# A fused decoder block: first loads on two queues, x's rows ahead of mem's, mem's squares on DVE, the position bias's product in the warm-up

## The chip, the cores and the metric

The kernel runs on one core of one Trainium2 chip. Its time is device microseconds of one execution; the median of three runs is what counts. A core has five engines that run their own instruction streams and wait for each other by semaphores: TensorE (PE, matrix products), VectorE (DVE), ScalarE (ACT), GpSimd (POOL) and SyncE (SP, which here only issues DMAs). ACT and POOL can issue DMAs too, on queues of their own.

## The reference

One layer of a decoder for 256 tokens of width 1024 (all float32). Only its beginning matters here: the memory's normed rows feed one product for keys and values, and the table of position biases is made from `rel_bias`.

```python
h = rmsnorm(x, g_pre_mix[l])
proj = h @ w_in[l]
(cb, cc, cv, q, k, v, qm, ga, gb, gc) = jnp.split(proj, IN_OFFSETS, axis=-1)
y_a = (cb * causal_dwconv(cc * cv, conv_mix_w[l])) @ w_conv_out[l]
o = moba_attention(to_heads(q), to_heads(k), to_heads(v), rel_bias)   # logits + bias of the distance
y_c = memory_attention(qm, rmsnorm(mem, g_mem[l]), w_mem_kv[l]) @ w_mem_out[l]
...                                                                   # gated merge, w_out, sandwich norm
u = causal_dwconv(h @ w_up[l], ffn_conv_w[l], ffn_conv_b[l])
f = (jax.nn.gelu(a) * g) @ w_down[l]
```

## The kernel before

Every float32 operand of a product is split in two parts, a rounded high part (ACT writes it, `wh`, or the first half of `memT`, `hT`, `mv`, `mk`) and the rest (DVE writes it, `wl`, or the second half). A product then takes three matmuls: high by high, high by low, low by high. The weights stream from DRAM in pieces of at most 128 x 1024 in the order in which they are used (`weight_pieces`); `split_until(n)` splits the pieces up to n, which first loads them, and `weights()` hands out the next one. Pieces w0 to w7 are the eight 128 x 512 slices of the memory's value weights, w8 to w11 the four column blocks of its key weights (128 x 1024 each), w12 to w15 the value weights of x.

The start, up to about 50 us, runs as follows.

- PE warms up on a constant (`keep_warm`, `pw`). The transposed memory `memT_in` is loaded into `rawT`, scaled by its gain `gm` and split (`mem_part`, `memT`), and `values` multiplies it with w0 to w7 into `pmv`: 48 matmuls. The memory's norm is applied afterwards, when `pmv` is copied out to `mv`, since it is one number for each token.
- The rows of `mem` and `x` (`m_sb`, `x_sb`, two tiles of 128 tokens each) are loaded for their norms alone. `rstd_full` squares and sums a row on ACT, in two halves (line 279, `junk`), and POOL adds them and takes the power -1/2 (lines 282 to 284), which gives `rm` and `rx`.
- `blocks` multiplies `memT` with w8 to w11 into two tiles `ft`, two blocks of 24 matmuls to a tile: blocks 0 and 1 in the first, 2 and 3 in the second. The keys' norm runs along the free axis, so `diagonals` puts `rm` on a diagonal (`dg`), a product with ones spreads it over all partitions (`sp`), and DVE copies it out as `rms`.
- `xn` is x times `rx`; PE turns it (`tp`), ACT and DVE scale and split it (`hT`), and `values` multiplies it with w12 to w15 into `pv`.
- The position bias: `bk`, a table of 33 x 384 with a one for the bucket of each distance, times `rb` gives `pb` (line 467); DVE copies it to `brow`, POOL writes it to DRAM (`bd`) and reads it back in a skewed form (`bias`), which the attention needs from about 73 us on.

The order of the work on PE, ACT and DVE up to the split of w11 and the order of the loads on SP's queue are written out by hand (`manual_schedule`); behind that a scheduler orders each engine's instructions when the kernel is built. SP issues its loads strictly in order, and each load first waits until the one eight places before it has landed.

Of the kernel before, what the change touches and what calls it, by code (L numbers as in the profile page):

```python
# [19 lines left out]
P = 128  # L20
# [4 lines left out]
H = 8  # L25
# [75 lines left out]
def trunk(ctx, tc, x, mem, memT_in, weights_in, par_in, rel_bias, g_post_mix, g_post_ffn, buckets, out):  # L101
# [28 lines left out]
    rawT = sb.tile([P, KT, S], F32, tag="G", name="rawT")  # L130
    par = const.tile([P, 60 + 8 * NFB], F32, name="par")
    gm, gp, gf, bg, cw = par[:, 0:8], par[:, 8:16], par[:, 16:24], par[:, 24:48], par[:, 48:60]
    fw = par[:, 60:].rearrange("p (a b) -> p a b", a=2)
    bk = sb.tile([P, 1024], F32, tag="z", name="bk")[:NB + 1, :TOEP]
    with tc.manual_schedule(engines={mybir.EngineType.Activation}):
        nc.scalar.dma_start(par[:, :8], par_in[:, :8])
    rb = const.tile([NB + 1, H], F32, name="rb")
    ident = const.tile([P, P], F32, name="ident")
    ones = const.tile([P, P], F32, name="ones")
# [147 lines left out]
    def rstd_full(src, name):  # L287
        return list(mean_square([src[:, :512], src[:, 512:]], name))[-1]

    def diagonals(rs):  # L290
        dg = wk.tile([P, NT, P], F32, tag="dg", name="dg", bufs=1)
        for t in range(NT):
            nc.vector.tensor_scalar_mul(dg[:, t], ident, rs[t])
        return dg

    def spread(dg, name):

        p = bank("sp")
# [91 lines left out]
    memT = sb.tile([P, 2, KT, S], F32R, tag="A", name="memT")  # L390
    mv = sb.tile([P, 2, NT, CW], F32R, tag="E", name="mv")
    pv = acc("pmv")

    def values(pv, a, k, wh, wl):
        for t in range(NT):
            mm_ktile([(pv[t], 0)], wh, wl, a[:, 0, k, tok(t)], a[:, 1, k, tok(t)], k == 0, k == KT - 1)

    with tc.manual_schedule(engines={mybir.EngineType.SP}):
        for what in "m01 w0 m12 w1 m24 w2 w3 m46 w4 w5 m68 w6 w7 w8 t0 w9 t1 x0 w10 x1 w11 w12 w13".split():
            if what[0] == "m":  # L400
                ks = slice(int(what[1]), int(what[2]))
                nc.sync.dma_start(rawT[:, ks], memT_in[:, ks])
            elif what[0] == "w":
                load(int(what[1:]), int(what[1:]))
            else:
                t = int(what[1])
                nc.sync.dma_start((x_sb if what[0] == "x" else m_sb)[:, t], (x if what[0] == "x" else mem)[tok(t)])
        nc.sync.dma_start(par[:, 8:], par_in[:, 8:])
        nc.sync.dma_start(rb[:NB], rel_bias)
        nc.sync.dma_start(bk, buckets)  # L410
    with tc.manual_schedule(engines={mybir.EngineType.PE, mybir.EngineType.Activation, mybir.EngineType.DVE}):
        nc.scalar.activation(small("preload"), mhalf, AF.Exp)
        pw = bank("pw")

        def keep_warm(n):
            one = nc.const_aps.tensor(1.0, (P, 512), BF16)
            for _ in range(n):
                nc.tensor.matmul(pw, one[:, :P], one, start=True, stop=True)

        def mem_part(k):  # L420
            hilo(memT[:, 0, k], memT[:, 1, k], rawT[:, k], gm[:, k:k + 1])

        keep_warm(9)
        for k in range(2):
            mem_part(k)
# [37 lines left out]

    pb = bank("pb")
    nc.tensor.matmul(pb[:H, :TOEP], rb, bk, start=True, stop=True)
    brow = wk.tile([H, TOEP], F32, tag="e", name="brow", bufs=EB)
    nc.vector.tensor_copy(brow, pb[:H, :TOEP])
    bd = dr.tile([H, TOEP], F32, name="bd")  # L470
# [382 lines left out]
```

## Time and profile before

| | us |
|---|---|
| median of 3 runs | 450.21 (449.69 to 450.3) |
| the profiled execution, its own time | 449.86 |
| its span, first to last instruction | 448.1 |
| PE busy | 435.7 (97%) |
| DVE busy | 358.2 (80%) |
| ACT busy | 292.4 (65%) |
| POOL busy | 15.6 (3%) |
| mean granted TensorE clock | 0.997 |

The span is what the trace covers; 1.76 us of the execution lie around it. Lines such as L256 are those of the kernel printed above.

### The profile page before, as it was taken

How to read it: one execution, taken by the hardware profiler on the slowest of the kernel's cores; microseconds unless marked ns; L12 is line 12 of the kernel's file. 1: busy time of each engine (PE TensorE's matmuls, PEld its weight loads, DVE VectorE, ACT ScalarE, POOL GpSimd, SP SyncE). 2: the span in 40 equal slices, each digit the busy share in tenths (PEclk: the TensorE clock that was granted, in tenths of full speed). 3: DMA queues.
4: the chain of work that ended last, by engine and by line, in shares of the span. 5: the costliest groups of instructions: out<-in, count | busy, mean ns of one | idle time of the engine just before them, and what ended most of it. 6: DMA issues, size and time to landing. Idle time of an engine off the chain costs nothing.

```text
span 448.1 us, 6694 instructions
## 1 busy us (share of the span) xinstructions
PE 435.7 (97%) x2425; PEld 375.7 (84%) x2425; DVE 358.2 (80%) x635; ACT 292.4 (65%) x533; POOL 15.6 (3%) x40
## 2 busy tenths in 40 slices
PE   7999999999999999999999899999999999999993
PEld 4797888888888998888888698888888888888882
DVE  4687789969987788698777579997878878788875
ACT  5984776756687776675655468866657657657642
POOL 0212000000000000000000300000000000000001
PEclk9999999999999999999999999999999999999998
DMA  7994765534535443555767036555556546546102
GB/s 241 411 407 178 245 225 187 187 114 171 187 105 190 176 144 140 187 177 195 249 225 279 5 140 236 189 187 191 193 182 198 189 176 203 189 176 209 70 1 94
DMA packets 14828, 83.45 MB, mean 186 GB/s; under 512 B 1827, under 2 KB 2636, under 8 KB 6092
## 3 DMA queue, kind: packets, MB, share of 16 engines
q1 hardware_dynamic: 14060, 80.92, 50.9%
q10 hardware_dynamic: 432, 1.05, 0.8%
q0 software_dynamic: 304, 1.06, 0.7%
q8 instruction: 19, 0.31, 0.3%
q14 instruction: 13, 0.11, 0.1%
HBM read 81.96 MB, written 1.06 MB: 185 GB/s over the span
## 4 chain that ended last, share of the span: by engine, by line
PE 91%; ACT 2%; DVE 1%; issue 1%; POOL 0%; POOLq 0%; DVEq 0%; ACTq 0%
PE ft L242 42%; PE ft L244 21%; PE pf L256 13%; PE po L256 5%; PE pv L256 2%; PE po L261 1%; ACT wh L216 1%; ACT junk L279 1%; PE at L261 1%; PE tp L312 0%; PE ft L233 0%; PE ft L378 0%; PE ft L234 0%; PE ft L374 0%; PE ft L235 0%
## 5 line engine op out<-in xcount | busy, mean ns | idle before, releaser
L216 ACT ACTIVATE wh<-raw 128x1024 fp32r<-128x1024 f32 (+1 forms) x139 | 143.1, 1033 | 104.3 <-PE ft L242 66.8
L217 DVE TENSOR_TENSOR wl<-raw,wh 128x1024 fp32r<-128x1024 f32 (+1 forms) x139 | 165.2, 1192 | 55.6 <-ACT wh L216 53.0
L242 PE MATMUL ft<-hT,wh 128*128 128x512 f32 x384 | 97.2, 393 | 0.0
L242 PE MATMUL ft<-h2T,wh 128*128 128x512 f32 x328 | 82.2, 392 | 0.0
L242 PEld LDWEIGHTS ft<-hT,wh 128*128 128x128 f32 x384 | 69.0, 189 | 12.2
L242 PEld LDWEIGHTS ft<-h2T,wh 128*128 128x128 f32 x328 | 59.5, 189 | 11.0
L244 PEld LDWEIGHTS ft<-hT,wl 128*128 128x128 f32 x384 | 52.2, 190 | 3.6
L244 PE MATMUL ft<-hT,wl 128*128 128x256 f32 x384 | 53.6, 282 | 0.0
L249 ACT ACTIVATE t<-ft 128x256 f32<-128x256 f32 x116 | 43.0, 372 | 10.4 <-PE ft L244 10.3
L256 PE MATMUL pf<-wh,f 128*128 128x512 f32 x176 | 49.2, 390 | 0.0
L244 PEld LDWEIGHTS ft<-h2T,wl 128*128 128x128 f32 x328 | 44.9, 190 | 3.3
L244 PE MATMUL ft<-h2T,wl 128*128 128x256 f32 x328 | 45.9, 282 | 0.0
L256 PEld LDWEIGHTS pf<-wh,f 128*128 128x128 f32 x176 | 32.4, 188 | 6.2
L250 DVE TENSOR_TENSOR y<-ft,t 128x256 f32<-128x256 f32 x68 | 28.2, 418 | 2.9 <-ACT t L249 2.6
L256 PE MATMUL pf<-wl,f 128*128 128x512 f32 x88 | 27.5, 390 | 0.0
L745 ACT ACTIVATE u<-v,par 128x256 f32<-128x256 f32 x44 | 24.0, 589 | 3.8 <-DVE v L739 3.7
L594 DVE SCALAR_TENSOR_TENSOR u<-v,par,u 128x255 f32<-128x255 f32 x44 | 19.7, 477 | 0.7 <-ACT u L745 0.7
L595 DVE SCALAR_TENSOR_TENSOR u<-v,par,u 128x254 f32<-128x254 f32 x44 | 19.6, 476 | 0.1
L256 PEld LDWEIGHTS pf<-wl,f 128*128 128x128 f32 x88 | 16.5, 188 | 3.5
L250 DVE TENSOR_TENSOR v<-ft,t 128x256 f32<-128x256 f32 x44 | 17.9, 417 | 0.5 <-ACT t L249 0.5
L256 PE MATMUL po<-wh,mg 128*128 128x512 f32 x64 | 17.9, 389 | 0.0
L282 POOL TENSOR_SCALAR se<-ss 128x1 f32<-128x1 f32 x10 | 3.4, 344 | 404.7 <-ACT junk L279 404.6
(172 smaller groups left out, 549.3 us busy)
## 6 DMA issues: line engine op xcount, KB each, us to landing
raw<-in_weights_dram SPq DMA_DIRECT2D x66, 1024.0 KB, 4.8
raw<-in_weights_dram SPq DMA_DIRECT2D x8, 256.0 KB, 5.7
rawx<-in_weights_dram SPq DMA_DIRECT2D x4, 512.0 KB, 10.2
rawx<-in_weights_dram SPq DMA_DIRECT2D x2, 1024.0 KB, 9.7
raw<-in_weights_dram SPq DMA_DIRECT2D x2, 512.0 KB, 6.9
m_sb<-in_mem_dram SPq DMA_DIRECT2D x2, 512.0 KB, 7.4
x_sb<-in_x_dram SPq DMA_DIRECT2D x2, 512.0 KB, 9.6
bias<-bd POOLq DMA_DIRECT2D x1, 1024.0 KB, 6.1
```

Of the source, the lines that this page charges most:

```text
L216: nc.scalar.activation(hi, v, AF.Copy)
L217: nc.vector.tensor_tensor(lo, v, f32(hi), ALU.subtract)
L242: nc.tensor.matmul(p, wh[:, k], a[:, :, k], start=(k == 0), stop=False)
L244: nc.tensor.matmul(p[:, :S], wl[:, k], a[:, 0, k], start=False, stop=(k == kt - 1))
L249: nc.scalar.activation(t, p[:, S:], AF.Copy)
L250: nc.vector.tensor_tensor(dst, p[:, :S], t, ALU.add)
L256: nc.tensor.matmul(d, a, w[:, c:c + 512], start=(first and w is wh and a is ah), stop=(last and a is al))
L261: nc.tensor.matmul(dst, a[i], b[j], start=(first and n == 0), stop=(last and n == 2))
L279: nc.scalar.activation(junk, src, AF.Square, scale=D ** -0.5, accum_out=q)
L594: nc.vector.scalar_tensor_tensor(t[:, 1:], src[:, :S - 1], w1, t[:, 1:], op0=ALU.mult, op1=ALU.add)
L595: nc.vector.scalar_tensor_tensor(t[:, 2:], src[:, :S - 2], w0, t[:, 2:], op0=ALU.mult, op1=ALU.add)
L745: nc.scalar.activation(d, v[:, i], AF.Identity, bias=bb, scale=w2)
```

## The change

- **First loads.** SP's queue no longer begins with `rawT`. The gain `gm` and the transposed memory are one array now, `gmT`; ACT's queue loads its first two pieces (`gm` with k-tiles 0 and 1, then 2 and 3), while SP's queue begins with w0 to w3. `bk` and `rb` move from the end of SP's list to POOL's queue, ahead of the identity.
- **Order of the rows.** x's first tile is loaded behind w8 and its second behind w9, where mem's tiles were; mem's follow them.
- **Norms.** `rstd_row` makes one sum over all 1024 columns. For x ACT does it, for mem DVE (`tensor_tensor_reduce`); POOL needs two instructions instead of three. `xn` is made in the hand-written part.
- **Bias product.** `pb` is computed straight after the warm-up, and `brow` is copied in the hand-written part.
- **First k-tile.** DVE also writes the high part of `memT`'s k-tile 0, and its six matmuls are reordered, so that low parts come last.
- **`spread`** is called when the first `ft` tile is copied out, not ahead of `blocks`; `pb` takes a pair of `acc` banks.

```diff
-        nc.scalar.dma_start(par[:, :8], par_in[:, :8])
+        for a, b in ((0, KT + 2 * S), (KT + 2 * S, KT + 4 * S)):
+            nc.scalar.dma_start(gmT[:, a:b], memT_in[:, a:b])
...
     with tc.manual_schedule(engines={mybir.EngineType.Pool}):
+        nc.gpsimd.dma_start(bk, buckets)
+        nc.gpsimd.dma_start(rb[:NB], rel_bias)
         make_identity(nc, ident)
...
+    def rstd_row(src, name, by_dve):
+        ss, se, r = small("ss"), small("se"), small(name)
+        junk = wk.tile([P, D], F32, tag="pT", name="junkd", bufs=2)
+        if by_dve:
+            nc.vector.tensor_tensor_reduce(junk, src, src, 1.0 / D, 0.0, ALU.mult, ALU.add, ss)
+        else:
+            nc.scalar.activation(junk, src, AF.Square, scale=D ** -0.5, accum_out=ss)
+        nc.gpsimd.tensor_scalar(se, ss, EPS, None, op0=ALU.add)
+        nc.gpsimd.tensor_tensor(r, se, mhalf, op=ALU.pow)
+        return r
...
-        for what in "m01 w0 m12 w1 m24 w2 w3 m46 w4 w5 m68 w6 w7 w8 t0 w9 t1 x0 w10 x1 w11 w12 w13".split():
+        for what in "w0 w1 w2 w3 m46 w4 w5 m68 w6 w7 w8 x0 w9 x1 t0 w10 t1 w11 w12 w13".split():
...
-        nc.sync.dma_start(par[:, 8:], par_in[:, 8:])
-        nc.sync.dma_start(rb[:NB], rel_bias)
-        nc.sync.dma_start(bk, buckets)
+        nc.sync.dma_start(par, par_in)
...
         keep_warm(9)
-        for k in range(2):
-            mem_part(k)
-            split_until(k + 1)
+        pb = acc("pb")[0]
+        nc.tensor.matmul(pb[:H, :TOEP], rb, bk, start=True, stop=True)
+        nc.vector.tensor_scalar_mul(memT[:, 0, 0], rawT[:, 0], gm[:, 0:1])
+        nc.vector.scalar_tensor_tensor(memT[:, 1, 0], rawT[:, 0], gm[:, 0:1], f32(memT[:, 0, 0]), op0=ALU.mult,
+                                       op1=ALU.subtract)
+        split_until(1)
+        mem_part(1)
+        split_until(2)
...
-        split_until(9)
-        rm = [rstd_full(m_sb[:, 0], "rm")]
-        split_until(10)
-        rm.append(rstd_full(m_sb[:, 1], "rm"))
-        rx = [rstd_full(x_sb[:, 0], "rx")]
+        rx, rm = [], []
+        for t in range(NT):
+            split_until(9 + t)
+            rx.append(rstd_row(x_sb[:, t], "rx", False))
+            rm.append(rstd_row(m_sb[:, t], "rm", True))
+            nc.vector.tensor_scalar_mul(xn[:, t], x_sb[:, t], rx[t])
         split_until(11)
-        rx.append(rstd_full(x_sb[:, 1], "rx"))
-        split_until(12)
+        nc.vector.tensor_copy(brow, pb[:H, :TOEP])
...
     def mk_evac(b, p):
         y = wk.tile([P, 2, S], F32, tag="y", name="y", bufs=YB)
-        nc.vector.tensor_tensor(y, two(p), twice(rms), ALU.mult)
+        if not rms:
+            rms.append(spread(diagonals(rm), "rms"))
+        nc.vector.tensor_tensor(y, two(p), twice(rms[0]), ALU.mult)
```

In the list of loads, m01 is a pair of k-tiles of the transposed memory, w0 a weight piece, t0 and x0 the row tiles of mem and x.

On DVE, from the split of w8 (`wl_246`) to the copy `rms`, the instructions before stand like this (`wl_268` is w9, `wl_298` is w10):

```order
L217 TENSOR_TENSOR wl_246<-raw_117,wh_245 128x1024
L293 TENSOR_SCALAR dg_323<-ident_82,rm_263 128x128
L217 TENSOR_TENSOR wl_268<-raw_117,wh_267 128x1024
L269 SCALAR_TENSOR_TENSOR mv_97<-pmv0_98,rm_263,mv_97 128x512
L293 TENSOR_SCALAR dg_323<-ident_82,rm_279 128x128
L269 SCALAR_TENSOR_TENSOR mv_97<-pmv1_99,rm_279,mv_97 128x512
L456 TENSOR_SCALAR xn_357<-x_sb_72,rx_291 128x1024
L217 TENSOR_TENSOR wl_298<-rawx_123,wh_297 128x1024
L302 COPY rms_329<-sp_326 128x256
```

With the change, from mem's first sum of squares (`junkd_268`; the row under it stores the sum) to the split of w11, the same place reads so (`wl_274` is w9, `wl_295` is w10, `wl_307` is w11):

```order
L298 ISA junkd_268,ss_265<-m_sb_73 128x1024
L298 ISA ss_265 128x1
L463 TENSOR_SCALAR xn_104<-x_sb_72,rx_260 128x1024
L221 TENSOR_TENSOR wl_274<-raw_119,wh_273 128x1024
L308 TENSOR_SCALAR dg_364<-ident_83,rm_267 128x128
L298 ISA junkd_287,ss_284<-m_sb_73 128x1024
L298 ISA ss_284 128x1
L463 TENSOR_SCALAR xn_104<-x_sb_72,rx_279 128x1024
L221 TENSOR_TENSOR wl_295<-rawx_125,wh_294 128x1024
L465 COPY brow_103<-pb0_147 8x384
L308 TENSOR_SCALAR dg_364<-ident_83,rm_286 128x128
L221 TENSOR_TENSOR wl_307<-rawx_125,wh_306 128x1024
```

and goes on to the copy `rms` (`wl_336` is w12, `wl_395` is w13):

```order
L273 SCALAR_TENSOR_TENSOR mv_100<-pmv0_101,rm_267,mv_100 128x512
L273 SCALAR_TENSOR_TENSOR mv_100<-pmv1_102,rm_286,mv_100 128x512
L221 TENSOR_TENSOR wl_336<-rawx_125,wh_335 128x1024
L466 TENSOR_SCALAR bgh_98<-par_75 128x24
L221 TENSOR_TENSOR wl_395<-rawx_125,wh_394 128x1024
L317 COPY rms_370<-sp_367 128x256
```

Before, three splits and `mv`'s two parts stood ahead of the copy `rms`; now five splits stand behind or between the two sums of squares and ahead of it, with `brow` and both tiles of `xn`. A sum of squares waits for its tile of mem to land, and w9's split, which block 1 needs, now stands behind it.

On PE, the end of block 1 (`wh_267`, `wl_268`: w9) and the start of block 2 (`wh_297`: w10) before:

```order
L233 MATMUL ft_332<-memT_96,wh_267 128x256
L234 MATMUL ft_332<-memT_96,wh_267 128x256
L235 MATMUL ft_332<-memT_96,wl_268 128x256
L300 MATMUL sp_326<-dg_323,ones_83 128x128
L312 MATMUL tp_393<-ident_82,xn_357 128x128
L312 MATMUL tp_394<-ident_82,xn_357 128x128
L233 MATMUL ft_415<-memT_96,wh_297 128x256
L234 MATMUL ft_415<-memT_96,wh_297 128x256
```

and with the change, from the first transpose behind block 1 to block 2 (`wh_294` is w10, `wh_335` and `wl_336` are w12):

```order
L327 MATMUL tp_376<-ident_83,xn_104 128x128
L327 MATMUL tp_377<-ident_83,xn_104 128x128
L327 MATMUL tp_376<-ident_83,xn_104 128x128
L327 MATMUL tp_377<-ident_83,xn_104 128x128
L327 MATMUL tp_376<-ident_83,xn_104 128x128 x2
L327 MATMUL tp_377<-ident_83,xn_104 128x128 x2
L315 MATMUL sp_367<-dg_364,ones_84 128x128
L260 MATMUL pv0_483<-wh_335,hT_375 128x512
L260 MATMUL pv1_484<-wh_335,hT_375 128x512
L260 MATMUL pv0_483<-wl_336,hT_375 128x512
L260 MATMUL pv1_484<-wl_336,hT_375 128x512
L237 MATMUL ft_398<-memT_99,wh_294 128x256
```

Six more transposes, the second `sp` and four matmuls of `pv` moved ahead of block 2. The tile `ft_398` of blocks 2 and 3 is given the PSUM bank in which `sp_367` was, as `ft_415` was given that of `sp_326` before: block 2 can't start until DVE has copied `rms` out of it.

## Rows read from the trace of the kernel before

**Rows 1.** Page, part 1: busy time, share of the span, instructions

```profile
PE 435.7 (97%) x2425; PEld 375.7 (84%) x2425; DVE 358.2 (80%) x635; ACT 292.4 (65%) x533; POOL 15.6 (3%) x40
```

**Rows 2.** Chain of waits, 0 to 110 us: start, us, what

```profile
25.24 0.96 ACT wh L216
...
26.25 0.36 PE ft L233
...
29.49 1.09 PE tp L312 x10
...
37.43 0.74 PE pb L467 x2
...
85.85 0.25 PE ft L242
```

**Rows 3.** Timeline of PE: start, length, line, operation, [idle before <- releaser]

```profile
5.96 0.50 PE L256 MATMUL pmv<-wh,memT 128*128 128x512 f32 x1 [1.20 <-ACT wh L216]
...
17.76 0.39 PE L256 MATMUL pmv<-wh,memT 128*128 128x512 f32 x1
19.06 0.49 PE L300 MATMUL sp<-dg,ones 128*128 128x128 f32 x2 [0.91 <-DVE dg L293]
...
25.36 0.38 PE L312 MATMUL tp<-ident,xn 128*128 128x128 f32 x2
...
33.17 0.40 PE L256 MATMUL pv<-wh,hT 128*128 128x512 f32 x1
33.40 0.40 PE L256 MATMUL pv<-wl,hT 128*128 128x512 f32 x1
```

**Rows 4.** Timeline of ACT

```profile
16.21 0.63 ACT L279 ACTIVATE junk<-m_sb 128x512 bf16<-128x512 f32 x1
...
22.77 1.05 ACT L216 ACTIVATE wh<-rawx 128x1024 fp32r<-128x1024 f32 x1
```

**Rows 5.** Timeline of DVE

```profile
18.92 1.22 DVE L217 TENSOR_TENSOR wl<-raw,wh 128x1024 fp32r<-128x1024 f32 x1
21.10 0.75 DVE L269 SCALAR_TENSOR_TENSOR mv<-pmv,rm,mv 128x512 fp32r<-128x512 f32 x1 [0.96 <-ACT mv L265]
21.77 0.28 DVE L293 TENSOR_SCALAR dg<-ident,rm 128x128 f32<-128x128 f32 x1
...
25.70 0.41 DVE L302 COPY rms<-sp 128x256 f32<-128x256 f32 x1
26.51 0.75 DVE L456 TENSOR_SCALAR xn<-x_sb,rx 128x1024 f32<-128x1024 f32 x1 [0.40 <-POOL rx L284]
...
30.65 0.17 DVE L441 TENSOR_SCALAR bgh<-par 128x24 f32<-128x24 f32 x1
30.73 1.22 DVE L217 TENSOR_TENSOR wl<-rawx,wh 128x1024 fp32r<-128x1024 f32 x1
...
39.96 0.54 DVE L469 COPY brow<-pb 8x384 f32<-8x384 f32 x1
```

**Rows 6.** Groups by form: line engine op, count | busy us, mean ns

```profile
L539 DVE CUSTOM_DVE_ANT_0 e<-sc,bias 128x256 f32<-128x256 f32 x8 | 3.4, 419 | 0.0
...
L539 DVE CUSTOM_DVE_ANT_0 e<-sc,bias 128x128 f32<-128x128 f32 x8 | 2.2, 279 | 0.0
```

**Rows 7.** Timeline of SP's queue, around 20 us

```profile
20.04 0.34 SPq L410 DMA_DIRECT2D bk<-in_buckets_dram  x1
```

**Rows 8.** Waits of SP's queue, 0 to 60 us: total, times, longest

```profile
SPq L410 <- DMA x_sb<-in_x_dram: 0.9, 1, 0.9
```

**Rows 9.** DMA, 0 to 60 us in 40 slices: busy tenths, GB/s

```profile
DMA  0579999999999999999999999500002988929999
GB/s 0 127 173 331 298 341 343 404 414 418 407 410 418 399 418 410 395 371 398 431 421 415 404 415 426 229 11 11 8 0 63 289 344 199 421 82 279 426 284 404
```

**Rows 10.** Timeline of POOL

```profile
19.63 0.59 POOL L282 TENSOR_SCALAR se<-ss 128x1 f32<-128x1 f32 x1 [0.95 <-ACT junk L279]
```

**Rows 11.** DMA issues, 0 to 60 us: KB each, us to landing

```profile
bd<-brow POOLq DMA_DIRECT2D x1, 12.0 KB, 3.2
```

More of the change, by code (lines that the diff above doesn't have):

```diff
@@ L128, in trunk @@
     m_sb = sb.tile([P, NT, D], F32, tag="E", name="m_sb")
[L130 to L133, printed above, removed]
+    gmT = sb.tile([P, KT + KT * S], F32, tag="G", name="gmT")
+    gm, rawT = gmT[:, :KT], gmT[:, KT:].rearrange("p (k s) -> p k s", s=S)
+    par = const.tile([P, 52 + 8 * NFB], F32, name="par")
+    gp, gf, bg, cw = par[:, 0:8], par[:, 8:16], par[:, 16:40], par[:, 40:52]
+    fw = par[:, 52:].rearrange("p (a b) -> p a b", a=2)
     bk = sb.tile([P, 1024], F32, tag="z", name="bk")[:NB + 1, :TOEP]
     with tc.manual_schedule(engines={mybir.EngineType.Activation}):
-        nc.scalar.dma_start(par[:, :8], par_in[:, :8])
+        for a, b in ((0, KT + 2 * S), (KT + 2 * S, KT + 4 * S)):
+            nc.scalar.dma_start(gmT[:, a:b], memT_in[:, a:b])
     rb = const.tile([NB + 1, H], F32, name="rb")
@@ L392, in trunk @@
     pv = acc("pmv")
+    brow = wk.tile([H, TOEP], F32, tag="e", name="brow", bufs=EB)
+    xn = sb.tile([P, NT, D], F32, tag="G", name="xn")
     def values(pv, a, k, wh, wl):
@@ L398, in trunk @@
     with tc.manual_schedule(engines={mybir.EngineType.SP}):
-        for what in "m01 w0 m12 w1 m24 w2 w3 m46 w4 w5 m68 w6 w7 w8 t0 w9 t1 x0 w10 x1 w11 w12 w13".split():
+        for what in "w0 w1 w2 w3 m46 w4 w5 m68 w6 w7 w8 x0 w9 x1 t0 w10 t1 w11 w12 w13".split():
             if what[0] == "m":
-                ks = slice(int(what[1]), int(what[2]))
-                nc.sync.dma_start(rawT[:, ks], memT_in[:, ks])
+                a, b = (KT + int(c) * S for c in what[1:])
+                nc.sync.dma_start(gmT[:, a:b], memT_in[:, a:b])
             elif what[0] == "w":
@@ L423, in trunk @@
         keep_warm(9)
-        for k in range(2):
-            mem_part(k)
-            split_until(k + 1)
+        pb = acc("pb")[0]
[6 more added lines that the diff above has]
+        split_until(2)
         for k in range(KT):
             wh, wl = weights(ahead=1)
-            values(pv, memT, k, wh[:, 0], wl[:, 0])
+            if k == 0:
+                for n, (a, w) in enumerate(((0, wh), (1, wh), (0, wl))):
+                    for t in range(NT):
+                        nc.tensor.matmul(pv[t], memT[:, a, 0, tok(t)], w[:, 0], start=(n == 0), stop=False)
+            else:
+                values(pv, memT, k, wh[:, 0], wl[:, 0])
             if k + 2 < KT:
@@ L432, in trunk @@
                 split_until(k + 3)
-        split_until(9)
-        rm = [rstd_full(m_sb[:, 0], "rm")]
-        split_until(10)
-        rm.append(rstd_full(m_sb[:, 1], "rm"))
-        rx = [rstd_full(x_sb[:, 0], "rx")]
+        rx, rm = [], []
+        for t in range(NT):
+            split_until(9 + t)
+            rx.append(rstd_row(x_sb[:, t], "rx", False))
+            rm.append(rstd_row(m_sb[:, t], "rm", True))
+            nc.vector.tensor_scalar_mul(xn[:, t], x_sb[:, t], rx[t])
         split_until(11)
-        rx.append(rstd_full(x_sb[:, 1], "rx"))
-        split_until(12)
+        nc.vector.tensor_copy(brow, pb[:H, :TOEP])
     nc.vector.tensor_scalar_mul(bgh, bg, 0.5)
@@ L443, in trunk @@
         hilo(mv[:, 0, t], mv[:, 1, t], pv[t], rm[t])
-    rms = spread(diagonals(rm), "rms")
+    rms = []
     mk = sb.tile([P, 2, HM, S], F32R, tag="mk", name="mk")
@@ L453, in trunk @@
     next(gen)
-    xn = sb.tile([P, NT, D], F32, tag="G", name="xn")
-    for t in range(NT):
-        nc.vector.tensor_scalar_mul(xn[:, t], x_sb[:, t], rx[t])
     next(gen)
@@ L462, in trunk @@
     run(gen)
[L466 to L469, printed above, removed]
     bd = dr.tile([H, TOEP], F32, name="bd")
-    nc.gpsimd.dma_start(bd, brow)
     bias = sb.tile([P, H, S], F32, tag="bias", name="bias")
-    nc.gpsimd.dma_start(bias, bass.AP(tensor=bd.tensor, offset=bd.offset + 1, ap=[[1, P], [TOEP, H], [1, S]]))
     vk = sb.tile([P, 4, 1024], F32R, tag="A", name="vk")
@@ L478, in trunk @@
     kl = vk[:, 2:].rearrange("p j (n s) -> p j n s", s=S)
-    for j, r in enumerate((slice(0, DH), slice(DH, P))):
-        nc.gpsimd.memset(f32(kl[r, 1 - j]), 0.0)
+    with tc.manual_schedule(engines={mybir.EngineType.Pool}):
+        for j, r in enumerate((slice(0, DH), slice(DH, P))):
+            nc.gpsimd.memset(f32(kl[r, 1 - j]), 0.0)
+        nc.gpsimd.dma_start(bd, brow)
+        nc.gpsimd.dma_start(bias, bass.AP(tensor=bd.tensor, offset=bd.offset + 1, ap=[[1, P], [TOEP, H], [1, S]]))
     pv = acc("pv")
@@ L831 @@
         "mem": whole("mem"),
-        "memT": tiles(whole("mem").T),
+        "memT": np.concatenate([per_feature(whole("g_mem")), tiles(whole("mem").T).reshape(P, KT * S)], axis=1),
         "weights": np.concatenate([tiles(w[name][k0 * P:(k0 + kt) * P, c0:c0 + n]).reshape(P, kt * n)
@@ L835 @@
         "par": np.concatenate([per_feature(whole(name)) for name in (
-            "g_mem", "g_pre_mix", "g_pre_ffn", "b_gate", "conv_mix_w", "ffn_conv_w", "ffn_conv_b")], axis=1),
+            "g_pre_mix", "g_pre_ffn", "b_gate", "conv_mix_w", "ffn_conv_w", "ffn_conv_b")], axis=1),
         "rel_bias": whole("rel_bias"),
```

## The prediction

> **What bounds the kernel now.** The busy times come first: PE is busy 97% of the span [rows 1], so a change is worth what it does to PE's waits or to PE's work. The chain of waits says where those waits are: from block 2's first matmul at 26.25 us to 86.10 PE runs without a gap, and what stands ahead of 26.25 on that chain is ACT [rows 2]. So the change is decided by when PE gets to block 2 and by what it has done by then. In PE's timeline the reader should see three losses ahead of it: 1.20 us before the first matmul of `pmv` at 5.96, 0.91 before `sp` at 19.06, and the gap behind the transposes that start at 25.36 [rows 3].
>
> The releaser of that last gap has to be read twice. The chain names an ACT split that runs from 25.24 [rows 2], but block 2 uses w10, whose high part was written at 22.77 to 23.82 [rows 4]. What ended just then is another thing: DVE's copy `rms`, 25.70 to 26.11 [rows 5], which empties the PSUM bank that block 2 writes. So block 2 starts 0.14 us behind that copy. The new order leaves this tie in place and puts much more work on DVE ahead of the copy; the prediction rests on that.
>
> **The change, part by part.** *The point of comparison.* With the change PE has done more when it reaches block 2: the bias product, 0.74 us; six more transposes at 0.109, 0.65 [rows 2]; four matmuls of `pv` at 0.23, 0.92 [rows 3]. Together 2.31, so the point that answers to 26.25 is 28.56: if block 2 starts later than that the kernel is slower by the difference, as long as PE has no new gaps behind it. I expect none: DVE will have split w13 before block 2 starts, at about 31.5, and before it was done with w13 at 30.73 + 1.22 = 31.95 [rows 5] with PE already further on.
>
> *DVE's chain.* The first new instruction that can be late is mem's first sum of squares, which waits for the tile t0. Everything DVE does behind it up to `rms` is in one line, and DVE starts the next instruction 0.08 us before one ends (21.10 + 0.75 against 21.77 [rows 5]), so each counts its length less 0.08:
>
> - the two sums of squares. The trace has no such instruction on 1024 columns. The nearest is line 539's reduction of two inputs, 0.279 on 128 columns and 0.419 on 256 [rows 6], 0.14 for each 128; an estimate for 1024 is 1.26. With 0.09 for storing the sum (as the smallest instruction here, 0.17 less 0.08 [rows 5]) that is 1.27 each, 2.54. The lower bound is the speed of `xn`, which goes over 1024 columns in 0.75 [rows 5]: 0.76 each. I take 1.27, since line 539 is the same kind of instruction;
> - both tiles of `xn`, 0.67 each, 1.34; five splits (w9 to w13) at 1.14, 5.70; two `dg` at 0.20, 0.40; two parts of `mv` at 0.67, 1.34; `brow` 0.46; `bgh` 0.09; `rms` 0.41 in full [rows 5].
>
> The sum is 12.28, and 0.14 to PE: block 2 starts 12.4 us after t0 lands. Nothing else is later: t1 lands two loads of 0.52 MB behind t0, 2.5 us at the 410 GB/s of that stretch [rows 9], and DVE reaches its sum 3.28 after t0.
>
> *When t0 lands.* Ahead of it, and with it, the new list has the memory, w0 to w9, both tiles of x and t0; the old list had just as many bytes up to x's first tile. That tile landed at about 20.0: SP's issue of `bk` at 20.04 waited for it [rows 7, 8]. The two queues at the start can only shift this. In the first 4.5 us the DMA engines stand idle for 1.5 us before anything moves, and then for a half, 0.3 and 0.1 of three slices [rows 9]: at most 1.35 us more could be filled, and nothing at the least. I take 0.5, because they are over half busy already when the loads flow: t0 at 19.5, between 18.65 and 20.0.
>
> The Trainium skill, "DMA: Bandwidth & Descriptors", section "Issuing engines are not separate DMA queues", says that DMAs of all issuing engines run on the same 16 engines and that more issuers save only the issue time. By it the gain would be the two issues that leave SP's queue, 0.34 each [rows 7], so 0.7, t0 at 19.3 and a sum 0.2 lower.
>
> *The sum.* Block 2 starts at 19.5 + 12.4 = 31.9, 3.3 us later than 28.56. The profiled execution took 449.86, so 453.2; the median of the runs shown lies 0.35 above it, which makes **453.5 us**.
>
> *What this makes worth nothing.* The early gains are all ahead of a wait. PE's own work from `pmv`'s first matmul to block 2 is 48 matmuls at 0.23, 11.0; the two blocks with `sp`, 6.3 (19.06 to 25.36); eight transposes and the four of `pv`, 1.8: 19.1 us [rows 2, 3]. So `pmv` could begin as late as 12.8 without moving block 2. The bias product in the warm-up is covered by PE's gap from 4.77 to 5.96 if its two loads have landed: the small load of POOL's queue here took 3.2 us [rows 11]. If they are slower its price is still nothing until 12.0. The same holds for k-tile 0's new order and the loads of w0. ACT's squares, eight halves of 0.63 [rows 4], become two whole rows; ACT was the engine that PE waited for through `rm` and `rx`, and now it waits itself, for loads and for `rm`. The skewed bias is read from about 73 us on and stays hidden.
>
> **The rivals.**
>
> *Faster: t0 comes early enough.* Then the removed waits count: `pmv` from 5.5 (4.77 and the bias product), block 2 at 24.6, 4.0 us ahead of 28.56: 446.2 us. This decides from t0 at 16.1 on (28.56 less 12.4). For it speaks that both queues fill from the start. Against it, t0 would need to be 3.9 us earlier with the same bytes ahead, and the engines show nine tenths from 4.5 us on [rows 9]. Chance 0.07.
>
> *No difference: the delay is given back later.* If PE waited somewhere behind for something that isn't late, such as a weight load, the 3.3 us would vanish there: 450.2. But the chain shows no wait up to 86.10 [rows 2], and behind it PE's waits are its own norms. Cheap sums of squares (0.76) with t0 at 18.65 also come near: block 2 at 30.0, 451.7, outside. Chance 0.09.
>
> *Slower still: POOL and DVE hold each other up.* One addition on POOL took 0.59 us, from 19.63 to 20.22, while DVE's split ran from 18.92 to 20.14 [rows 5, 10]: it seems to have ended only when the split did. No row shows DVE waiting for POOL. But four POOL instructions (for both `rm`) now fall into DVE's unbroken line, and at 0.59 each they would add up to 2.4: block 2 at 34.3, 455.9. Chance 0.10. The Trainium skill, "SBUF — State Buffer", section "SBUF: two separate sides", describes this as a shared pair of ports that the instruction that starts first holds to its end, and so in either direction; the trace agrees for POOL's side (0.59), and no row shows the other.
>
> **How the numbers follow.** The forecast, DVE's line sets block 2 and PE runs on from there, gets 0.74. Its own bounds: t0 0.85 earlier and sums at 0.76 take off 1.9, 451.6; t0 at 20.0 and half of POOL's 2.4 add 1.7, 455.2. The range 451.4 to 455.2 holds that and a part of the last rival, and leaves out 0.07 + 0.09 and some 0.04. A measurement of this kernel can tell about 0.2%, 0.9 us, from no change. Slower by more than that: 0.74 + 0.10 = 0.84; within it 0.09; faster 0.07.
>
> **What would show it.** In the profile after, DVE should be idle ahead of the first sum of squares for two to three microseconds, released by the DMA of `m_sb` at about 19.5, and then not idle until `rms`, near 31.7. PE should have its first matmul near 5.6, a wait for w9's low part near 21 to 22.7, then waits at `pv` and ahead of block 2, about 5 us in all from 20 to 32, and none to 86. ACT should be idle between 18 and 25. The prediction is wrong if t0 lands before 18, if the sums of squares are shorter than 0.8, or if block 2 doesn't wait for the copy `rms`.

## The result

| | before | after |
|---|---|---|
| median, us | 450.25 (449.69 to 450.39, 4 runs) | **454.49** (453.87 to 455.22, 4 runs) |
| profiled execution: span / time, us | 448.1 / 449.86 | 452.4 / 454.33 |

The ratio is 1.0095, 95% interval 1.0079 to 1.0111: 4.24 us slower, where 3.3 were forecast (453.5, range 451.4 to 455.2). PE has the same share of the span as in [rows 1]; POOL, with fewer instructions, is busy for 4 us more.

```profile
PE 437.6 (97%) x2425; PEld 377.5 (83%) x2425; DVE 361.1 (80%) x640; ACT 289.2 (64%) x520; POOL 19.6 (4%) x38
```

PE's timeline after shows where the time went. It answers to [rows 3]:

```profile
0.76 3.68 PE L433 MATMUL pw<-const-bfloat16-1.0 128*128 128x512 bf16 x9 [0.76 <-PEq L863]
7.95 1.44 PE L440 MATMUL pb<-bk,rb 33*8 33x384 f32 x2 [3.51 <-DMA rb<-in_rel_bias_dram]
9.32 2.07 PE L452 MATMUL pmv<-wh,memT 128*128 128x512 f32 x4
...
28.39 0.39 PE L315 MATMUL sp<-dg,ones 128*128 128x128 f32 x2
28.61 1.04 PE L327 MATMUL tp<-ident,xn 128*128 128x128 f32 x8
29.48 0.39 PE L315 MATMUL sp<-dg,ones 128*128 128x128 f32 x2
30.89 0.73 PE L260 MATMUL pv<-wh,hT 128*128 128x512 f32 x2 [1.03 <-ACT hT L269]
31.82 0.73 PE L260 MATMUL pv<-wl,hT 128*128 128x512 f32 x2 [0.20 <-DVE wl L221]
33.38 0.39 PE L237 MATMUL ft<-memT,wh 128*128 128x256 f32 x1 [0.82 <-DVE rms L317]
```

PE waits 3.51 us for `rb`, and `pmv` begins at 9.3 instead of 5.96. From 7.95 to the end of block 1 there is no gap. Then come three waits, 2.05 us together: for `hT`'s high part from ACT, for a weight's low part, and 0.82 for the copy `rms`, behind which block 2 starts at 33.38. From there on PE is busy to past 60. Stretches of the same execution show a second loss at the start. A row gives the stretch and its length, PE's busy time with the number of matmuls, the granted clock, the DMA engines' share and GB/s:

```profile
4.00:8.00 4.00, 0.49 (x3) 0.92 1.00 359
8.00:14.00 6.00, 6.00 (x13) 0.50 1.05 398
14.00:34.00 20.00, 17.95 (x107) 0.99 1.03 413
```

PE was idle for 3.51 us, and then the granted clock is 0.50, the lower of the two levels (1.2 GHz), for 6 us: the bias product took 1.44 us (two matmuls from 7.95 to 9.39) where the kernel before has 0.74 [rows 2], and the first matmuls of `pmv` 0.47 each. At half clock those 6 us hold 3 us of work, so 3 were lost. In the kernel before PE waited 1.20 at this place [rows 3], and the granted clock of the same stretch is 1.00.

DVE's timeline after, against [rows 5]:

```profile
18.49 1.23 DVE L221 TENSOR_TENSOR wl<-raw,wh 128x1024 fp32r<-128x1024 f32 x1 [1.11 <-ACT wh L220]
19.63 1.22 DVE L298 CUSTOM_DVE_ANT_0 junkd<-m_sb 128x1024 f32<-128x1024 f32 x1
20.78 0.08 DVE L298 DVE_READ_ACCUMULATOR2_ANT ss<- 128x1 f32 x1
21.31 0.75 DVE L463 TENSOR_SCALAR xn<-x_sb,rx 128x1024 f32<-128x1024 f32 x1 [0.46 <-POOL rx L302]
...
23.67 0.29 DVE L308 TENSOR_SCALAR dg<-ident,rm 128x128 f32<-128x128 f32 x1 [0.47 <-POOL rm L302]
23.87 1.22 DVE L298 CUSTOM_DVE_ANT_0 junkd<-m_sb 128x1024 f32<-128x1024 f32 x1
...
25.55 0.75 DVE L463 TENSOR_SCALAR xn<-x_sb,rx 128x1024 f32<-128x1024 f32 x1 [0.45 <-POOL rx L302]
...
32.91 0.42 DVE L317 COPY rms<-sp 128x256 f32<-128x256 f32 x1
```

From the first square at 19.63 to the end of `rms` at 33.33 are 13.70 us. The squares take 1.22 and 0.08 for the read, as priced. What the sum did not have are three waits for POOL, 0.46, 0.47 and 0.45. POOL's timeline says why:

```profile
19.89 1.39 POOL L302 TENSOR_TENSOR rx<-se,mhalf 128x1 f32<-128x1 f32 x1
...
22.23 1.40 POOL L302 TENSOR_TENSOR rm<-se,mhalf 128x1 f32<-128x1 f32 x1
...
24.12 1.40 POOL L302 TENSOR_TENSOR rx<-se,mhalf 128x1 f32<-128x1 f32 x1
...
26.47 1.40 POOL L302 TENSOR_TENSOR rm<-se,mhalf 128x1 f32<-128x1 f32 x1
```

Each power took 1.39 to 1.40 us, and each ended about 0.43 behind the end of the square or split beside which it ran. In kernels where DVE runs nothing beside it, it takes 0.57 (below).

The load of `rb`, issued from POOL's queue at 2.05, landed 5.77 us later, at 7.82 (chain of waits of the same run):

```profile
2.05 5.77 DMA rb<-in_rel_bias_dram
7.82 0.14 issue
7.95 1.44 PE pb L440 x2
```

### The profile page after: what moved, and what is told of

The parts are those of the page before. It is cut to its first block, busy times and chain, and to the rows that moved or that the text cites. A ratio compares the mean times of both kernels' runs of the same rounds, so it can differ in the third digit from the quotient of the medians.

```text
span 452.4 us, 6670 instructions
## 1 busy us (share of the span) xinstructions
PE 437.6 (97%) x2425; PEld 377.5 (83%) x2425; DVE 361.1 (80%) x640; ACT 289.2 (64%) x520; POOL 19.6 (4%) x38
## 4 chain that ended last, share of the span: by engine, by line
PE 94%; DVE 2%; DMA 1%; ACT 1%; issue 1%; POOL 0%; POOLq 0%; DVEq 0%; ACTq 0%
PE ft L246 41%; PE ft L248 21%; PE pf L260 13%; PE po L260 5%; PE pmv L260 2%; PE pv L260 2%; PE po L265 1%; DMA rb<-in_rel_bias_dram 1%; PE ft L237 1%; PE ft L238 1%; PE ft L239 1%; DVE wl L221 1%; PE pmv L452 1%; PE at L265 1%; PE tp L327 1%
## 5 line engine op out<-in xcount | busy, mean ns | idle before, releaser
L286 POOL TENSOR_SCALAR se<-ss 128x1 f32<-128x1 f32 x6 | 1.9, 319 | 391.2 <-ACT junk L283 391.1
## 6 DMA issues: line engine op xcount, KB each, us to landing
rawx<-in_weights_dram SPq DMA_DIRECT2D x2, 1024.0 KB, 12.8
```

## The experiments

Three theories are tested: **D**, DVE's line holds the copy `rms`, and block 2 is tied to that copy because it takes `sp`'s bank (the prediction). **P**, PE's late and slow start sets block 2. **G**, POOL's powers stretch DVE's line. In the expectations PE is TensorE, DVE VectorE, ACT ScalarE and POOL GpSimd. Differences are to the runs of the kernel before on the same chip, whose median was 450.11, 450.09 and 449.96 in the three groups of kernels.

**First group: parts undone, one at a time**

*mem's squares on ACT.* This and the other experiments start from the changed kernel, unless the kernel before is named.

```
-            rm.append(rstd_row(m_sb[:, t], "rm", True))
+            rm.append(rstd_row(m_sb[:, t], "rm", False))
```

> The changed kernel with mem's two sums of squares given back to ScalarE, 1024 columns at once like those of x. Theory D (VectorE's line from mem's first row tile to the copy rms holds block 2 of mk's product, and nothing else does): the line loses two squares of 1.26, block 2 starts 2.5 us or more earlier, about 30.5, and the time falls by 2.5 to 4.2, to 450.3 to 452.0. Theory D+P (VectorE's line, and under it TensorE's late and slow start, which alone would put block 2 at about 30.5 against 28.56): the time falls only by the part above that floor, 2.5 to 3, to 451.5 to 452.3, and TensorE is dense from 8 to block 2. Theory P (the late start alone): no change, 454.2 to 454.8.

Measured: 451.77, +1.66 (ratio 1.0039, 1.0027 to 1.0052). Block 2 starts at 29.71, and of the waits ahead of it one of 0.61 is left. That is D+P of the expectation: DVE's line was the larger part, and something below it holds the rest. POOL's four powers now take 0.57 each; mem's first is this one, at a time when DVE is idle:

```profile
20.66 0.57 POOL L302 TENSOR_TENSOR rm<-se,mhalf 128x1 f32<-128x1 f32 x1
```

*The bias product put back.* Its loads go to the end of SP's list, matmul and `brow` behind mk's product:

```
     with tc.manual_schedule(engines={mybir.EngineType.Pool}):
-        nc.gpsimd.dma_start(bk, buckets)
-        nc.gpsimd.dma_start(rb[:NB], rel_bias)
...
-        pb = acc("pb")[0]
-        nc.tensor.matmul(pb[:H, :TOEP], rb, bk, start=True, stop=True)
...
     run(gen)
+    pb = bank("pb")
+    nc.tensor.matmul(pb[:H, :TOEP], rb, bk, start=True, stop=True)
+    nc.vector.tensor_copy(brow, pb[:H, :TOEP])
```

> The changed kernel with the bias product alone put back: its two loads behind all others on SP's queue, the matmul and the copy brow after mk's product. TensorE's wait of 3.5 us for rb's load and its low clock behind it should go, mem's product starting near 5.5 instead of 9.4. Theory D: block 2 still waits for rms, which hangs on mem's rows and VectorE's line; the time stays within 0.5 of the changed kernel's, or rises by the 0.74 of the product that is back on TensorE's path, 454.2 to 455.2. Theory P: the floor falls by 2 and more, and the time with it, 451.5 to 453.

Measured: 455.98, +5.87 (1.0130, 1.0116 to 1.0143), above what either theory gave. `pmv` begins at 6.06, but block 2 only moves to 32.72: P alone is out. What is lost beyond that goes with the clock. PE, early now, stands idle ahead of block 2, and then:

```profile
27.59 0.49 PE L313 MATMUL sp<-dg,ones 128*128 128x128 f32 x2 [1.01 <-DVE dg L306]
30.24 0.81 PE L258 MATMUL pv<-wh,hT 128*128 128x512 f32 x2 [2.16 <-ACT hT L267]
...
32.72 0.58 PE L235 MATMUL ft<-memT,wh 128*128 128x256 f32 x1 [0.33 <-DVE rms L315]
...
33.53 0.41 PE L235 MATMUL ft<-memT,wh 128*128 128x256 f32 x1
```

```profile
26.00:30.00 4.00, 1.07 (x8) 1.00 1.01 401
...
31.00:37.00 6.00, 5.54 (x23) 0.50 1.01 415
```

PE worked 1.07 us of the four from 26 to 30; from 31 to 37 the clock is 0.50 and a block's matmul is listed at 0.41 instead of 0.28. Here an earlier PE that had to wait lost more than one that came late. (Its start was slow as well: behind 1.88 us of idle time ahead of `pmv` the clock is 0.50 from 8 to 10.)

*Without POOL's instructions.* One addition on DVE stands for both; the power -0.5 is left out.

```
-        nc.gpsimd.tensor_scalar(se, ss, EPS, None, op0=ALU.add)
-        nc.gpsimd.tensor_tensor(r, se, mhalf, op=ALU.pow)
+        nc.vector.tensor_scalar(r, ss, EPS, None, op0=ALU.add)
```

> The changed kernel with GpSimd's two instructions for each row tile replaced by one addition on VectorE; the power -0.5 is left out, so the rows are scaled by their mean square and not by its root. Theory G (GpSimd's powers, 1.39 each beside VectorE's two-input work, hold VectorE up three times by 0.46): VectorE's line falls by 1.4 less four additions of 0.07, block 2 comes near 32.2 and the time falls by about 1.1, to 453.2 to 453.6. Rival (VectorE's idle 0.46 is covered by another wait, that for mem's second row tile or for ScalarE's x squares): no change, 454.2 to 454.8.

Measured: 452.06, +1.95 (1.0044, 1.0030 to 1.0058): 2.3 less than the changed kernel, twice the 1.1 that the expectation gave to G. DVE's line:

```profile
18.97 0.15 DVE L301 TENSOR_SCALAR rx<-ss 128x1 f32<-128x1 f32 x1
19.04 1.22 DVE L298 CUSTOM_DVE_ANT_0 junkd<-m_sb 128x1024 f32<-128x1024 f32 x1
...
31.01 0.40 DVE L316 COPY rms<-sp 128x256 f32<-128x256 f32 x1
```

From 19.04 to 31.41 are 12.37 us, three additions of 0.07 among them: without POOL the line has about the length that the prediction summed (12.28). Block 2 starts at 31.47, 1.91 earlier than in the changed kernel: 1.32 of that is the shorter line, but 0.59 is the first square, which starts earlier (19.04 against 19.63) because the split ahead of it does. So not all of the 2.3 is POOL's.

*The loads on two queues alone, on the kernel before.*

```
-        nc.scalar.dma_start(par[:, :8], par_in[:, :8])
+        for a, b in ((0, KT + 2 * S), (KT + 2 * S, KT + 4 * S)):
+            nc.scalar.dma_start(gmT[:, a:b], memT_in[:, a:b])
...
-        for what in "m01 w0 m12 w1 m24 w2 w3 m46 ...".split():
+        for what in "w0 w1 w2 w3 m46 ...".split():
...
```

> The kernel before with the first part of the change alone: g_mem and the first four of mem's transposed tiles on ScalarE's queue, the weights from the start on SP's; norms, bias product and order of the rows of x and mem as before. If the early loads are what is late in the kernel before, everything up to block 2 comes earlier by what TensorE's first matmul gains, 0.3 to 0.7, and the time is 449.5 to 450.0. If mem's rows, which stand as deep in the sum of the bytes as before, set block 2: no change, 450.0 to 450.5. Theory that two queues in themselves cost (less of the bandwidth for the weights): 450.6 or more.

Measured: 450.32, no change (1.0005, 0.9996 to 1.0014). `pmv` starts at 6.66, 0.70 later than in the kernel before. Block 2 starts at 26.77, and here the profile itself names the copy `rms` as what it waits for (0.39), which is how the prediction read the rows of the kernel before.

**Second group: the two ties**

*PE kept busy up to the bias product.*

```
-        keep_warm(9)
+        keep_warm(17)
```

> The changed kernel with 17 warm-up matmuls for 9, eight of 0.41 more, so that TensorE is busy until rb has landed near 7.8 and its clock stays at the high level: mem's product then loses no time at half speed (3.2 in the changed kernel, from 7.7 to 14.1 at 0.50). Theory P (TensorE's late and slow start sets block 2): block 2 comes 2 to 3 earlier, 451.5 to 452.5. Theory D (VectorE's line sets it): block 2 stays within 0.5 of 33.4 and the time within 0.5 of the changed kernel's, 454.0 to 455.0; TensorE then stands idle for about 5 instead of 2 ahead of block 2, and if the clock falls for that as it did with the bias product put back (0.50 from 30.7 to 37.4, 3.3 lost), 455.5 to 457.

Measured: 452.93, +2.84 (1.0055, 1.0040 to 1.0069), between the theories. It isn't a pure test: in the order that the compiler wrote, `rms` now stands ahead of two splits, 1.14 each, that it followed before, and DVE's first square started at 18.97 instead of 19.63. So block 2 doesn't wait for `rms` here. PE waits 2.16 for `hT` instead, and in the profiled execution the clock is 0.57 from 30 to 34:

```profile
29.70 0.73 PE L260 MATMUL pv<-wh,hT 128*128 128x512 f32 x2 [2.16 <-ACT hT L269]
30.27 0.28 PE L237 MATMUL ft<-memT,wh 128*128 128x256 f32 x1
```

Block 2 comes 3.1 earlier, which is not D as the expectation put it, and a part is given back at the low clock. Of the six executions four took 452.87 to 453.32 at a mean granted clock of 0.991 or 0.992; two took 451.43 and 451.54 at 0.995. So the run shows that the start is worth something, and doesn't decide between the theories.

*`sp` in a bank of its own.*

```
-    def spread(dg, name):
+    def spread(dg, name, p=None):
-        p = bank("sp")
+        p = bank("sp") if p is None else p
...
-        pb = acc("pb")[0]
+        pb, spare = acc("pb")
...
-            rms.append(spread(diagonals(rm), "rms"))
+            rms.append(spread(diagonals(rm), "rms", spare))
```

> The changed kernel with the product sp written to the second bank of pb's pair, which nothing uses, so that block 2 takes no bank that the copy rms has to free; VectorE, ScalarE and GpSimd have the same work. Theory D as the prediction put it (block 2 waits for rms because of sp's bank): block 2 starts when its weights and TensorE are ready, 29 to 30, some 3.5 earlier, and what waits for VectorE next is the first product of hT's; the time falls by 2 to 3.5, to 451.0 to 452.5. Rival (the tie to rms only ends last of several: the scaled transposes hT or weights' low parts come as late): less than 1 falls, 453.6 to 454.6.

Measured: 450.93, +0.84 (1.0023, 1.0013 to 1.0032): 3.4 less. DVE has the same instructions, POOL's powers are as long, and `rms` ends as late (33.46) as in the changed kernel (33.33), but block 2 no longer asks for it. PE and then DVE (`sp` is listed as `pb` here, after the pair of banks that it is written to):

```profile
27.94 0.39 PE L315 MATMUL pb<-dg,ones 128*128 128x128 f32 x2
28.08 0.36 PE L237 MATMUL ft<-memT,wh 128*128 128x256 f32 x1
...
34.78 0.63 PE L260 MATMUL pv<-wh,hT 128*128 128x512 f32 x2
```

```profile
33.05 0.41 DVE L317 COPY rms<-pb 128x256 f32<-128x256 f32 x1
```

Block 2 follows `sp` at 28.08 and PE has no gap from 7.88 to past 60. That `sp`'s bank is what holds block 2 back is shown by this one edit. How the 3.4 divide is not: with the bank free the compiler also wrote another order. The four matmuls of `pv` that stood ahead of block 2 and waited 1.23 there (1.03 and 0.20) now stand behind block 3, at 34.78, and `hT`'s low parts stand ahead of `rms` on DVE. In the changed kernel the wait for `rms` itself was only 0.82. PE also reached `sp` earlier in this execution, at 27.94 instead of 28.39 and with two transposes more behind it.

*Squares on ACT and PE kept busy.*

```
-            rm.append(rstd_row(m_sb[:, t], "rm", True))
+            rm.append(rstd_row(m_sb[:, t], "rm", False))
...
-        keep_warm(9)
+        keep_warm(17)
```

> mem's squares on ScalarE and 17 warm-up matmuls. If what was left over the kernel before with the squares on ScalarE (1.66) is TensorE's slow start, mem's product ends 2 earlier here, block 2 starts near 27.5 and the time is 449.2 to 450.2, level with the kernel before. If it is GpSimd and the order of the norms, 451.4 to 452.2.

Measured: 450.32, +0.23 (1.0007, 0.9998 to 1.0015), level with the kernel before. DVE has the same order as with the squares on ACT alone, so this is a clean pair: of the 1.66 left there, 1.4 was PE's start.

*Squares on ACT, the bias product behind `pmv`'s second k-tile.*

```
-        keep_warm(9)
-        pb = acc("pb")[0]
-        nc.tensor.matmul(pb[:H, :TOEP], rb, bk, start=True, stop=True)
+        keep_warm(12)
...
+            if k == 1:
+                pb = acc("pb")[0]
+                nc.tensor.matmul(pb[:H, :TOEP], rb, bk, start=True, stop=True)
...
-            rm.append(rstd_row(m_sb[:, t], "rm", True))
+            rm.append(rstd_row(m_sb[:, t], "rm", False))
```

> mem's squares on ScalarE, the bias product behind the second k of mem's product instead of ahead of the first, where its load has long landed, and 12 warm-up matmuls, so that TensorE neither waits for rb nor loses its clock. If the start is what is left, mem's product starts near 6 and ends by 21, block 2 waits for rms at 26.5 to 28, and the time is 448.5 to 450.0, below or level with the kernel before. If the norms of mem behind those of x are what is left, 451 to 452.

Measured: 451.43, +1.34 (1.0018, 1.0008 to 1.0029), a miss. `pmv` starts at 6.01, but block 2 waits 1.93 for `rms` and starts at 28.23, as late as with the warm start (28.27). The twelve runs stand in two groups, five at 449.98 to 450.40 and seven at 451.41 to 452.04. The profiled one is of the upper, with a clock of 0.85 and 0.73 between 26 and 34; of the lower there is no trace. Their mean granted clocks point the same way (0.995 to 0.998 in the lower group, 0.991 to 0.995 in the upper), so that the clock is the difference is likely; no trace shows it.

**Third group: both ties, the order of the rows, and the kernel before**

*The changed kernel with `sp` in the spare bank and 17 warm-up matmuls.* Its edits are those of the two experiments above.

> The changed kernel, mem's squares on VectorE as it has them, with both ties taken away: sp in the spare bank of pb's pair and 17 warm-up matmuls. With the spare bank alone TensorE was busy without a gap from 7.9 on, and what it still had over the kernel before (0.84) is its late start and its slow first matmuls. If that is all, the warm start gives back what it gave with the squares on ScalarE, 1.4, and the time is 449.0 to 449.9, below the kernel before. If VectorE's line is the next to be waited for (through hT or the low parts), it stays at 450.5 to 451.2.

Measured: **448.66**, -1.30 (0.9971, 0.9959 to 0.9982), faster than both kernels. DVE still squares mem's rows, and ahead of the first square its timeline is what the prediction wanted to see:

```profile
19.84 1.23 DVE L298 CUSTOM_DVE_ANT_0 junkd<-m_sb 128x1024 f32<-128x1024 f32 x1 [2.73 <-DMA m_sb<-in_mem_dram]
...
33.35 0.42 DVE L317 COPY rms<-pb 128x256 f32<-128x256 f32 x1
```

It idles 2.73 us for t0, which lands at 19.8, and `rms` ends at 33.77, later than in the changed kernel, which is 5.5 us slower. A late `rms` costs nothing once PE doesn't wait for it.

*mem's rows first, squares on ACT, 17 warm-up matmuls.*

```
-        for what in "... w8 x0 w9 x1 t0 w10 t1 w11 w12 w13".split():
+        for what in "... w8 t0 w9 t1 x0 w10 x1 w11 w12 w13".split():
...
-        keep_warm(9)
+        keep_warm(17)
...
-            rx.append(rstd_row(x_sb[:, t], "rx", False))
-            rm.append(rstd_row(m_sb[:, t], "rm", True))
+            rm.append(rstd_row(m_sb[:, t], "rm", False))
+            rx.append(rstd_row(x_sb[:, t], "rx", False))
```

> mem's squares on ScalarE, 17 warm-up matmuls, and the rows of mem loaded and normed ahead of x's, as the kernel before has it; against the same kernel with x's rows ahead (450.32). If the order of the rows is part of the loss, rms is there some 2 earlier, block 2 loses its wait of 0.94 and the time is 449.2 to 449.8. If x's rows, then late, hold the transposes and hT's first product up by as much, 450.1 to 451.

Measured: 450.28, +0.32 (1.0006, 0.9997 to 1.0015), the same as with x's rows first (+0.23). Block 2 waits 1.14, and the releaser that the profile names has to be read twice again:

```profile
28.43 0.36 PE L237 MATMUL ft<-memT,wh 128*128 128x256 f32 x1 [1.14 <-ACT wh L220]
```

```profile
27.88 0.40 DVE L317 COPY rms<-sp 128x256 f32<-128x256 f32 x1
```

ACT wrote w10's high part from 23.86 on; what ends 0.15 ahead of block 2 is once more `rms`, at 28.28. It is no earlier than with x's rows first (28.13), since `xn`, w10's split and `brow` stand ahead of it on DVE. So with the squares on ACT and `sp` in its bank the order of the rows changes nothing, but an `rms` that comes 2 earlier, which the expectation asked about, was not tested.

*The kernel before with `sp` in another bank.*

```
-    def spread(dg, name):
+    def spread(dg, name, p=None):
-        p = bank("sp")
+        p = bank("sp") if p is None else p
...
-    rms = spread(diagonals(rm), "rms")
+    rms = spread(diagonals(rm), "rms", acc("sp")[0])
```

> The kernel before with one edit: sp in a bank of the accumulators' pool, so that block 2 takes no bank that rms frees. If the 0.5 ahead of block 2 in the kernel before is the same tie, block 2 follows block 1 without a gap and the time falls by 0.3 to 0.6, to 449.5 to 449.8; if something else comes as late there, 450.0 to 450.4.

Measured: 452.79, +2.83 (1.0055, 1.0042 to 1.0068), a miss on the other side; four of the five executions took 452.69 to 452.81, one 451.35. PE and then DVE:

```profile
27.14 0.44 PE L312 MATMUL tp<-ident,xn 128*128 128x128 f32 x2 [1.90 <-DVE xn L456]
...
28.27 0.58 PE L235 MATMUL ft<-memT,wl 128*128 128x256 f32 x1 [0.31 <-DVE wl L217]
28.65 0.41 PE L233 MATMUL ft<-memT,wh 128*128 128x256 f32 x1
```

```profile
25.27 0.42 DVE L302 COPY rms<-sp 128x256 f32<-128x256 f32 x1 [1.90 <-PE sp L300]
...
26.34 0.74 DVE L456 TENSOR_SCALAR xn<-x_sb,rx 128x1024 f32<-128x1024 f32 x1
```

PE waits 1.90 for `xn`, and then the matmuls are at 0.41 again. With the bank free the compiler wrote another order for DVE: `rms` and `y` stand ahead of x's first tile `xn`, which starts at 26.34 instead of 23.89 [rows 5], although its `rx` is there at 24.19; DVE stands idle for `sp` meanwhile. The two transposes ahead of block 2, which were there before, wait for it. So this run shows what the new order costs, and leaves open what the bank alone is worth in the kernel before.

*Squares on ACT, the bias product behind the second k-tile, 12 warm-up matmuls, `sp` in the spare bank.* The edits are shown above.

> mem's squares on ScalarE, the bias product behind the second k of mem's product with 12 warm-up matmuls, and sp in the spare bank: TensorE starts mem's product near 6 at full clock, as in the kernel before, waits for no rms, and has the bias product where it would wait for weights. If start and tie are the two causes of the loss, TensorE has no gap over 0.5 from 6 to 45 and the time is 447.8 to 449.3, below both kernels. If the wait moves on to hT's first product, as with the warm start alone (2.16 for ScalarE's hT, and the clock fell), 450 to 452.

Measured: 448.65, -1.31 (0.9971, 0.9960 to 0.9983), level with the kernel that leaves the squares on DVE. From 6.06 to past 45 PE has no wait above 0.45.

The four kernels that keep the squares on DVE make a table of the two ties (difference to the kernel before, us):

| | `sp` in `rms`'s way | `sp` in the spare bank |
|---|---|---|
| 9 warm-up matmuls, PE idle for 3.1 to 3.5 us ahead of the bias product | +4.24 (changed kernel) | +0.84 |
| 17 warm-up matmuls, idle for 0.6 to 1.5 us | +2.84 | **-1.30** |

By their medians the bank is worth 3.4 to 4.1, the start 1.4 to 2.1, each with the orders that the compiler wrote for it. The +2.84 holds a fall of the clock too: with its two faster executions, at about +1.4, the bank would be worth 2.7 there and the start 2.8.

## Why the prediction held, and where its terms were off

*Block 2 is tied to `rms` by `sp`'s bank.* Right, and the point on which all rests: the spare bank alone takes 3.4 us away with the same instructions on every other engine. That is the tie together with the order that the compiler builds around it; the two were not taken apart.

*DVE's line, 12.4 from the first square to block 2.* Measured 13.75. The instructions were priced right (12.37 against 12.28 with POOL out of the way). The missing 1.35 is the rival that was given 0.10, POOL and DVE holding each other up. It was priced at 2.4, four additions that stretch; what stretches most is the powers, and what counts is three waits of DVE's for their results, 1.38 in all. POOL's four powers run 1.39 to 1.40 instead of 0.57 where they stand beside a two-input instruction of DVE's. That the time falls by 2.3 without POOL is more than this, since the first square began 0.59 earlier in that run. No row shows a DVE instruction that itself grew: the two squares and the splits keep their 1.22. So one side is slowed and the other waits for its result. The Trainium skill, "SBUF — State Buffer", section "SBUF: two separate sides", says that whichever of the two starts first holds the shared ports to its end; the powers that stretch to 1.39 agree with that, and DVE being held likewise is not seen in these rows.

*t0 at 19.5.* Measured at 18.97, 19.49 and 19.84 in the kernels where DVE does wait for it (PE kept busy; bias product back; both ties away). The count of issues that leave SP's queue was one short: m01, m12 and m24 are three. In the changed kernel itself t0 landed at 18.8 (issued at 10.42, 8.4 to landing), and DVE came to the first square only at 19.63, from a split that was late, so the 2 to 3 us of idle time that I wanted to see ahead of it were not there. That 19.63 stands so near the 19.5 of the sum is luck: t0 was 0.7 earlier than taken, and DVE 0.8 later than t0.

*What was worth nothing.* This step failed as it was put. It let `pmv` begin as late as 12.8 and the bias product as late as 12.0; they began at 9.39 and 7.95, and yet the start costs 1.4 to 2.1. Two terms were missing. The load from POOL's queue was taken at 3.2 us from a row that is a store in a quiet stretch [rows 11], and took 5.77 while the weights came in; that the traffic is the reason was not tested. And PE's own work, 19.1 us, was counted at full clock, but 6 us of it ran at half after the wait. The late `pmv` also held ACT's splits back (it waited 2.17 us for a slot that PE had not freed), and through them DVE's first square, by up to 0.7 (19.63 against 18.97 with PE kept busy).

*The point of comparison, 28.56.* From there to the end of the span the kernel before has 448.1 - 28.56 = 419.54; the changed kernel has 452.4 - 33.38 = 419.02, the one without powers 450.4 - 31.47 = 418.93, and the one with ACT's squares, which has still 0.92 of `pv` to do at 29.71, 418.97. So the point should have stood 0.5 later, which is why 4.82 at block 2 came out as 4.24. About half of the 0.5 lies ahead of 260 us: PE's wait for `xs` comes at 254.57 before and at 259.13 after, so 2.57 had been done ahead of block 2 and not 2.31. The other half lies behind it (193.53 to the end before, 193.27 after). Which of the three parts of the 2.31 was short is open. The second `sp`, which the section on the change lists as moved, is none of them: it stood ahead of block 2 before too, at 25.14.

The terms together: 31.9 + 0.13 (first square) + 1.35 (POOL) = 33.38, less 0.5 behind it.

*The rivals.* t0 early enough: out; it needed 16.1, and t0 landed at 18.8 to 19.8. The delay given back: only 0.5 of it.

*The other signs.* Three that the prediction named did not show. PE had no wait for w9's low part; its waits ahead of block 2 were 2.05 and not 5, because it came late itself; and ACT was idle for only 1.5 of the 7 us from 18 to 25.

## What to carry to other kernels

Before giving an engine more work, ask which buffer its last instruction frees and who takes that buffer next: here a PSUM bank that was free elsewhere was worth 3.4 us, more than the choice of the engine for the squares (2.6). Where a compiler orders the instructions, a freed buffer also changes the order, for better or worse, so read the order again before giving a cause. A PE that is made to start earlier must also find its later inputs ready: in these runs idle times of 1.9 to 3.5 us were followed by stretches at half clock that cost one to three more. An edit that "hides" in a warm-up hides only if its load lands there under the traffic of that moment, so price it from a row of a busy stretch.

## What the runs showed of the hardware

- POOL's power on 128x1 takes 0.57 us alone and 1.39 to 1.40 beside DVE's two-input instructions on 1024 columns. An addition, 0.22 alone, took 0.78 beside `xn`, which reads one tile (from 21.36 to 22.14, with `xn` from 21.31 to 22.06).
- A small load of POOL's queue took 5.77 us to land between 2 and 8 us, while the DMA engines moved 177 GB/s (2 to 4 us) and then 359 (4 to 8), against 3.2 for a store, the 12 KB of `bd`, at 8 GB/s (39 to 45 us) [rows 11].
- The granted clock was 0.50 behind an idle time of 3.51 us in the changed kernel (8 to 14 us), behind 1.01 and 2.16 with the bias product put back (31 to 37), and behind 0.17 and 2.16 with PE kept busy (32 to 34). It stayed at 1.00 behind 1.03, 0.20 and 0.82 in the changed kernel, and behind 1.14 with mem's rows first.
- The clock row can miss such a stretch. With the squares on ACT it reads 1.00 all through, and yet six matmuls of `pmv` take 2.7 us from 9.25 on (0.45 each, where one takes 0.23 in the kernel before), as at half clock; the durations have to be read beside it:

```profile
7.88 1.44 PE L440 MATMUL pb<-bk,rb 33*8 33x384 f32 x2 [3.12 <-DMA rb<-in_rel_bias_dram]
9.25 2.07 PE L452 MATMUL pmv<-wh,memT 128*128 128x512 f32 x4
...
11.97 0.63 PE L260 MATMUL pmv<-wh,memT 128*128 128x512 f32 x1
```
